# Moving a block of transposes into an earlier phase, and letting two interleaved streams end in step

## The chip, the cores and the metric

The kernel runs on one core of one Trainium2 chip. The metric is the device time of one execution in microseconds (us). PE is the matmul engine, PEld its weight loads, ACT, DVE and POOL are the scalar, vector and GpSimd engines, SP is the engine that issues most of the transfers.

## The reference

One layer of a hybrid decoder, for a prompt of 1024 tokens and for 8 samples of 8 new tokens with 8192 cached positions each. Everything is 32-bit floating point.

```python
h = rmsnorm(x, g_pre_mix) * (1 + sc1) + sh1            # adaLN from c
z = h @ w_in                                           # q, k, v, r, gate of GLA; cq, ckv, kr of MLA
o_a = gla(q_a, k_a, v_a, log_a, s0)                    # gated linear attention, chunks of 64
cq  = rmsnorm(cq, g_mla_q);  ckv = rmsnorm(ckv, g_mla_kv);  kr = rope(kr)
q_nope, q_rope = split(cq @ w_mla_uq);  q_lat = q_nope @ w_mla_uk
s = q_lat . kv_all + q_rope . kr_all                   # causal; a sample: 8192 cached rows, then its 8
o_b = rmsnorm((softmax(scale * s) @ kv_all) @ w_mla_uv, g_mla_out)
x = x + gt1 * rmsnorm(concat(o_a, o_b) @ w_o, g_post_mix)
u = (rmsnorm(x, g_pre_ffn) * (1 + sc2) + sh2) @ w_ffn_up
x = x + gt2 * rmsnorm((conv(u)[a] * gelu(conv(u)[g])) @ w_ffn_down, g_post_ffn)
```

Outputs are both `x`, the new latent rows and rotary keys, the GLA states and the last rows of `u`.

## The kernel before

A matmul of full precision is split: each operand becomes a rounded high part (a cast on ACT, `split` and lines like it) and a low part (a subtraction, `lo`, L121, on DVE or POOL), and three matmuls (`mm3`, L140 to L142) take the place of one.

The program goes through these stages. `phase1` computes `z` for all tokens and stores its parts in scratch memory: the latent rows with their rotary keys in `s_kv` (prompt rows 0 to 1023, sample rows behind them), the query latents stay in SBUF as `cqT`. `sample_queries` makes the samples' queries. Then a mixed stage runs two streams together. `out_proj`, `ffn_up` and `ffn_down` follow it.

*The two streams of the mixed stage.* `run` hands two generators to `interleave` (L1665). The *sample stream* is `mla_sample`: for each of 8 samples, 4 rounds over 2048 cached rows. A round gathers two tiles `L` and two tiles `R` by indirect loads on POOL's queue, transposes them on PE (`kps`, L1222, 40 transposes, copied by ACT at L1224 into `KT` and `KR`), makes the scores `S` (L1232, L1234), takes a softmax on DVE and ACT (L1237 to L1255), transposes the probabilities on DVE (L1261) and multiplies them with `L` (`O`, L1266). The *main stream* is `main` in `run`: `prompt_queries`, then `gla`, then `mla_prompt`, then `out_weights`, which starts the loads of `w_o`.

*What sets the order.* A planner orders each engine's instructions. Each instruction has a priority, a number that counts up as the program is written down, and of those that can go, the lowest number goes first. `interleave` steps the generator that has done the smaller share of its total; a step yields its cost, and the totals are 429.0 for the sample stream and 250.0 for the main one. While it steps the sample stream it adds 450 to the running priority, so that a sample instruction stands as if 450 instructions later; for the main stream it adds 0. An engine's queue and SP's queue run in order: what stands behind a waiting instruction waits too.

*Prompt queries.* `prompt_queries` (L1000) takes tokens in blocks of 256, 256 and 320. `queries` first splits the block of `cqT` into `cqsh` and `cqsl` (`split_cq`, L890; the cast is L132, the subtraction L121 on POOL), with one buffer each, which the matmuls of the whole block read. After each step of the queries one step of `mla_new` follows, which attends to the samples' own 8 new rows; it has six steps, and the queries have 19.

*Prompt attention.* `mla_prompt` (L1029) opens three pools (`mk`, `mb`, `mv`) on the left-hand stack of SBUF where GLA's were, and begins with the keys: 8 times it loads 128 rows of `s_kv` into `kvl` (L1047, two buffers), transposes three 128 x 128 blocks on PE into one PSUM buffer (`pt`, L1050), casts them on ACT into `kTh` (L1051) and subtracts on DVE into `kTl` (L121). Each of these two tiles takes 12 KB of a partition. For each of 4 heads, `keys(h)` loads a part of `w_mla_uk` (`ukr`, L1066), splits it (`uks`, L1059) and makes K; `scores(h, m)` makes the scores of 256 queries (`sps`) and their exponentials `p` (four buffers of 4 KB); `values` transposes `p` on PE (`pt`, L1153), splits the result into `pth` (ACT, L1156) and `ptl` (DVE), and multiplies it with V (`olps`). `values` runs one `scores` behind, so that the last two `values` come after the last scores.

*The hand-over.* `out_weights` opens the pools `fw0` and `fw1` where the prompt attention's pools end, at the same base of the stack. `block` loads a quarter of `w_o` (1 MB) into `uraw` (L1383, two buffers of 8 KB, first in the pool), casts it on ACT into `uhi` (L1388) and subtracts on DVE into `ulo`; the first block's `uhi` and `ulo` come next in the pool. A tile can be written only when what lay at its addresses is done with. `out_proj` loads the mixed rows (`mx`, L1414), transposes them (`tps`, L1421) and multiplies them with the four blocks (`y`); after it come the blocks of `w_ffn_up`, which use the same two raw buffers.

Of the kernel before, what the change touches and what calls it, by code (L numbers as in the profile page):

```python
# [1 line left out]

# [1 line left out]

# [5 lines left out]
F32 = mybir.dt.float32  # L11
F32R = mybir.dt.float32r
# [8 lines left out]
P = 128  # L21
D = 1024
TP = 1024
# [82 lines left out]
class Kernel:  # L106
# [781 lines left out]
            self.lo(self.uk[1][:, o], p3, self.uk[0][:, o], nc.vector)  # L888

    def split_cq(self, c0, n, eng=None):  # L890
        return self.split(self.qp, self.cqT[:, :, c0:c0 + n], (3, 320), "cqs", eng, bufs=1, n=n)

    def queries(self, qp, pp, c0, n, rope, ql=None, cqs=None):

# [102 lines left out]
            except StopIteration as e:  # L997
                return e.value

    def prompt_queries(self):  # L1000

        new = self.mla_new(self.kp, self.nq, self.pq, self.qs, self.qrs)
        for c0, n in ((0, 256), (256, 256), (512, 320)):
            gen = self.queries(self.qp, self.pq, c0, n, self.ropet[:, c0 // P:])
            while True:
                try:
                    yield next(gen)
                except StopIteration as e:
                    self.store_queries(*e.value, c0, n)
                    break  # L1010
                next(new, None)
        for _ in new:
            pass
# [15 lines left out]
    def mla_prompt(self):  # L1029
        nc, A = self.nc, self.A  # L1030
        with ExitStack() as es:
            kp = es.enter_context(self.pool("mk"))
            bp = es.enter_context(self.pool("mb", bufs=1))
            mv = es.enter_context(self.pool("mv"))
            ep = self.ep
            psS = es.enter_context(self.pool("pss", bufs=2, space=PSUM))
            pq = es.enter_context(self.pool("psq", bufs=1, space=PSUM))
            causal = kp.tile([P, P], F32R, name="causal")
            craw = kp.tile([P, P], F32, name="craw")
            nc.sync.dma_start(craw, A["c_causal"])  # L1040
            nc.scalar.copy(causal, craw)
            kTh = kp.tile([P, 3, TP], F32R, name="kTh")
            kTl = kp.tile([P, 3, TP], F32R, name="kTl")
            for i in range(8):
                kv = bp.tile([P, 3, P], F32, name="kvl", tag="kvl", bufs=2)
                o = slice(i * P, (i + 1) * P)
                nc.sync.dma_start(kv.rearrange("p c k -> p (c k)"), self.s_kv[o])  # L1047
                ps = pq.tile([P, 3, P], F32, name="pt", tag="Q", bufs=1)
                for c in range(3):
                    nc.tensor.transpose(ps[:, c], kv[:, c], self.ident)  # L1050
                nc.scalar.copy(kTh[:, :, o], ps)  # L1051
                self.lo(kTl[:, :, o], ps, kTh[:, :, o], nc.vector)
                yield 0.4

            def split2(x, name):

                n = x.shape[2]
                t = bp.tile([P, TP], F32R, name=name, tag="pp", bufs=4)[:, 0:4 * n].rearrange("p (j a n) -> p j a n", j=2, a=2)
                nc.scalar.copy(t[:, 0], x)  # L1059
                self.lo(t[:, 1], x, t[:, 0], nc.vector)  # L1060
                return t
# [603 lines left out]
    def interleave(self, *gens):  # L1665

        live = [[0.0, total, g, ahead] for g, total, ahead in gens]
        while live:
            it = min(live, key=lambda x: x[0] / x[1])
            p = self.tc.cur_priority  # L1670
            try:
                self.tc.cur_priority = p + it[3]
                it[0] += next(it[2])
            except StopIteration:
                live.remove(it)
            self.tc.cur_priority -= it[3]


    def run(self, stop=None):
        nc = self.nc  # L1680
        with ExitStack() as es:
            dp = es.enter_context(self.pool("scratch", space=DRAM))
            self.s_kv = dp.tile([T, LAT + 2 * RO], F32, name="s_kv")
            self.s_qn = dp.tile([4, P, TP], F32, name="s_qn")
            self.s_qr = dp.tile([2, P, TP], F32, name="s_qr")
            self.s_qk = dp.tile([4, P, T], F32, name="s_qk")
            self.s_la = dp.tile([T, 256], F32, name="s_la")
            self.s_v = dp.tile([T, 512], F32, name="s_v")
            self.s_r = dp.tile([T, 512], F32, name="s_r")
            self.s_mix = dp.tile([T, D], F32, name="s_mix")  # L1690
            self.s_x2 = dp.tile([T, D], F32, name="s_x2")
            self.s_gate = dp.tile([2, 65, D], F32, name="s_gate")
            self.s_g = dp.tile([NCH, P, T], F32, name="s_g")
            self.s_ml = dp.tile([1, 512], F32, name="s_ml")
            self.cp = cp = es.enter_context(self.pool("const"))
            self.constants(cp)
            self.ada_start(cp)
            fs = es.enter_context(ExitStack())
            gs = es.enter_context(ExitStack())
            ds = es.enter_context(ExitStack())  # L1700
            with ExitStack() as zs, ExitStack() as xs:
                self.zp = zs.enter_context(self.pool("z"))
                self.xp = xs.enter_context(self.pool("x", bufs=2, side="right"))
                self.phase1()
                if stop == "z":
                    return
                with ExitStack() as es2:
                    self.sample_queries(zs, xs, ds, es2)
                    if stop == "q":
                        return  # L1710

                    def main():
                        yield from self.prompt_queries()
                        zs.close()
                        yield from self.gla()
                        yield from self.mla_prompt()
                        self.wp = [fs.enter_context(self.pool(f"fw{j}")) for j in range(2)]
                        self.gt = gs.enter_context(self.pool("gate"))
                        self.out_weights()
                        yield 0.0  # L1720

                    self.ep = es2.enter_context(self.pool("me", bufs=1, side="right"))
                    self.interleave((self.mla_sample(es2), 429.0, 450), (main(), 250.0, 0))
            if stop == "mix":
                return
            with ExitStack() as hs:
                with self.pool("pt", bufs=2, space=PSUM) as self.pt, self.pool("pu", space=PSUM) as self.pu:
                    hT = self.out_proj(hs, ds)
                    gs.close()
                    if stop == "wo":  # L1730
                        return
                    self.ffn_up(hT)
                    if stop == "up":
                        return
            self.ffn_down()
# [35 lines left out]
```

## Time and profile before

| | us |
|---|---|
| three runs of the kernel before | 1873.49, 1874.45, 1879.61 |
| their median | 1874.45 |
| the profiled execution | 1877.98 |
| its span, first to last instruction | 1876.2 |

The profile is of one execution. Its page has the busy time of each engine, the chain of work that ended last, and the costliest groups of instructions; its trace can be asked for stretches of time, for one tile, for waits, and for the instructions of one engine in order of time. Matmuls overlap in it, so that the times of single ones can't be added up; an engine's busy time counts overlaps once. The granted clock is a share of TensorE's full clock, 2.4 GHz; at half of it the engine runs at 1.2 GHz.

### The profile page before, as it was taken

What the parts mean: (1) busy time and instruction counts of PE and PEld (TensorE: products, weight loads), DVE (VectorE), ACT (ScalarE), POOL (GpSimd) and SP (SyncE); (2) the same over time, 40 slices, a digit from 0 to 9 for tenths busy, and PEclk for the clock granted to TensorE, in tenths of its full rate; (3) what the DMA queues carried; (4) which work ended last, traced back from release to release, by engine and by line L of the source; (5) the groups of instructions that cost most, each with busy time, mean ns of one, the idle gap of its engine ahead of it and who ended that gap; (6) DMA issues with size and microseconds to landing.
All of it is one profiled execution on the core that took longest, in us unless ns stands there. A gap on an engine that the chain in (4) does not pass through costs nothing.

```text
span 1876.2 us, 30747 instructions
## 1 busy us (share of the span) xinstructions
PE 1804.7 (96%) x12403; PEld 1501.0 (80%) x12403; DVE 933.5 (50%) x1680; ACT 709.3 (38%) x1398; POOL 528.5 (28%) x567
## 2 busy tenths in 40 slices
PE   6999999999998999999889999999999999999998
PEld 3888767766654677776589999999999999888787
DVE  4740234358873555565546855455555554623433
ACT  3451111465655667566523422222222222323322
POOL 2640100334443223232101223333333331202221
PEclk7999999999999999999989999999999999999999
DMA  8255653665556555455543312112211112834563
GB/s 308 75 163 181 195 159 100 216 212 189 174 194 213 174 191 179 141 167 192 180 147 116 131 64 71 70 69 71 69 56 64 69 62 71 255 110 115 159 188 95
DMA packets 170617, 265.26 MB, mean 141 GB/s; under 512 B 18277, under 2 KB 118693, under 8 KB 162282
## 3 DMA queue, kind: packets, MB, share of 16 engines
q1 hardware_dynamic: 156138, 179.39, 29.5%
q0 software_dynamic: 14336, 83.89, 12.9%
q8 instruction: 98, 1.61, 0.4%
q14 instruction: 45, 0.37, 0.1%
HBM read 221.49 MB, written 41.75 MB: 140 GB/s over the span
## 4 chain that ended last, share of the span: by engine, by line
PE 84%; DMA 6%; DVE 4%; ACT 4%; issue 1%; POOL 1%; SPq 0%; DVEq 0%; POOLq 0%; ACTq 0%
PE ups L140 9%; PE ups L142 9%; PE ups L141 9%; PE kps L1222 6%; PE yps L142 4%; PE yps L140 4%; PE yps L141 4%; PE zps L140 3%; PE zps L142 3%; PE zps L141 3%; PE O L1266 3%; PE S L1232 3%; PE y L140 2%; PE y L141 2%; PE y L142 2%; PE adaps L248 2%
## 5 line engine op out<-in xcount | busy, mean ns | idle before, releaser
L140 PE MATMUL ups<-gh,uhi 128*128 128x384 f32 (+1 forms) x1056 | 347.4, 329 | 0.3 <-DVE hraw L342 0.3
L141 PE MATMUL ups<-gl,uhi 128*128 128x384 f32 (+1 forms) x1056 | 346.9, 328 | 0.0
L142 PE MATMUL ups<-gh,ulo 128*128 128x384 f32 (+1 forms) x1056 | 346.7, 329 | 0.0
L1560 DVE TENSOR_SCALAR cv<-u,vt 128x1024 f32<-128x1024 f32 (+1 forms) x88 | 133.1, 1533 | 216.0 <-ACT u L1550 179.0
L140 PEld LDWEIGHTS ups<-gh,uhi 128*128 128x128 f32 x1056 | 198.4, 188 | 0.7 <-DVE hraw L342 0.6
L142 PEld LDWEIGHTS ups<-gh,ulo 128*128 128x128 f32 x1056 | 198.4, 188 | 0.1
L141 PEld LDWEIGHTS ups<-gl,uhi 128*128 128x128 f32 x1056 | 198.4, 188 | 0.0
L1224 ACT COPY KT<-kps 128x512 f32<-128x512 f32 x256 | 145.6, 590 | 84.0 <-PE kps L1222 82.4
L121 POOL TENSOR_TENSOR ulo<-uraw,uhi 128x2048 fp32r<-128x2048 f32 x24 | 111.4, 4641 | 207.5 <-ACT uhi L1388 204.7
L1222 PEld LDWEIGHTS kps<-ident,L 128*128 128x128 f32 x1024 | 113.3, 143 | 64.0 <-issue 43.3
L1222 PE MATMUL kps<-ident,L 128*128 128x128 f32 x1024 | 156.9, 283 | 7.9 <-ACT KT L1224 6.4
L1550 ACT COPY u<-ups 128x384 f32<-128x384 f32 (+1 forms) x130 | 57.6, 444 | 278.8 <-PE ups L142 278.8
L142 PE MATMUL yps<-uhi,gl 128*128 128x512 f32 x341 | 132.8, 390 | 5.0 <-DVE gl L121 5.0
L140 PE MATMUL yps<-uhi,gh 128*128 128x512 f32 x341 | 132.7, 389 | 0.0
L141 PE MATMUL yps<-ulo,gh 128*128 128x512 f32 x341 | 132.6, 389 | 0.0
L121 DVE TENSOR_TENSOR gl<-graw,gh 128x1408 fp32r<-128x1408 f32 x31 | 59.0, 1908 | 128.3 <-ACT gh L1607 128.3
L1213 POOL DMA_INDIRECT R<-cache_krope,idx x64 | 64.9, 1014 | 184.1 <-PE kps L1222 141.8
L1607 ACT CAST gh<-graw 128x1408 fp32r<-128x1408 f32 (+1 forms) x35 | 45.7, 1307 | 157.1 <-PE yps L141 127.6
L1388 ACT CAST uhi<-uraw 128x2048 fp32r<-128x2048 f32 (+1 forms) x38 | 70.7, 1864 | 89.7 <-PE ups L141 67.2
L1212 POOL DMA_INDIRECT L<-cache_latent,idx x64 | 63.6, 993 | 136.3 <-PE O L1266 63.7
L140 PE MATMUL zps<-whi,hh 128*128 128x512 f32 (+2 forms) x256 | 96.3, 376 | 0.0
L142 PE MATMUL zps<-whi,hl 128*128 128x512 f32 (+2 forms) x256 | 94.2, 368 | 0.8 <-DVE hl L121 0.8
(443 smaller groups left out, 3802.8 us busy)
## 6 DMA issues: line engine op xcount, KB each, us to landing
wraw<-w_ada SPq DMA_DIRECT2D x48, 512.0 KB
uraw<-w_ffn_up SPq DMA_DIRECT2D x22, 1024.0 KB
graw<-s_g SPq DMA_DIRECT2D x32, 704.0 KB
s_g<-gl SPq DMA_DIRECT2D x22, 544.0 KB
uraw<-w_ffn_down SPq DMA_DIRECT2D x10, 1024.0 KB
xt<-x_prompt SPq DMA_DIRECT2D x16, 512.0 KB
wraw<-w_in SPq DMA_DIRECT2D x12, 512.0 KB
uraw<-w_o SPq DMA_DIRECT2D x4, 1024.0 KB
```

Source lines behind the costliest of these rows:

```text
L121: eng.tensor_tensor(out, x, hi.bitcast(F32), ALU.subtract)
L140: mm(out, wh, xh, start=start, stop=False)
L141: mm(out, wh, xl, start=False, stop=False)
L142: mm(out, wl, xh, start=False, stop=stop)
L1212: nc.gpsimd.indirect_dma_start(L.rearrange("p j l -> p (j l)"), None, cl, io)
L1213: nc.gpsimd.indirect_dma_start(R.rearrange("p j l -> p (j l)"), None, ck, io)
L1222: nc.tensor.transpose(ps[:, k], x, self.ident)
L1224: nc.scalar.copy(KT[:, q // 2, j0:j0 + 4] if q < 4 else KR[:, 4 * half:4 * half + 4], ps)
L1232: nc.tensor.matmul(S[r], Q[:, c], KT[:, c, :, r], start=(c == 0), stop=False)
L1388: self.nc.scalar.copy(hi, raw)
L1550: copy(u[:, 2 + c0:2 + c0 + m], ps[:, 0:m])
L1560: nc.vector.tensor_scalar(yv[z], sh(2)[z], self.cw2[:, ch:ch + 1], self.cb[:, ch:ch + 1], ALU.mult, ALU.add)
```

## The change

The keys of the prompt attention become a generator of their own, `prompt_keys`, with the same loads, transposes, casts and subtractions. `prompt_queries` chains it behind `mla_new`, so that its eight tiles are written down among the steps of the queries, before GLA. `kTh` and `kTl` lie in a new pool `mkT` on the right-hand stack of SBUF, `kvl` in the pool of the queries (two buffers, as before), and the transposes use the four PSUM buffers of the queries instead of the one buffer of the prompt attention. `mla_prompt` starts with the keys of the first head. The split query latents get two buffers each. `interleave` scales what it adds to the priority by the share of the stream that is still to come: 450 at first, 0 at the end. The main stream's total becomes 244.5.

```diff
     def split_cq(self, c0, n, eng=None):
-        return self.split(self.qp, self.cqT[:, :, c0:c0 + n], (3, 320), "cqs", eng, bufs=1, n=n)
+        return self.split(self.qp, self.cqT[:, :, c0:c0 + n], (3, 320), "cqs", eng, bufs=2, n=n)
...
+    def prompt_keys(self, kp, bp, pq):
+        nc = self.nc
+        self.kTh = kp.tile([P, 3, TP], F32R, name="kTh")
+        self.kTl = kp.tile([P, 3, TP], F32R, name="kTl")
+        for i in range(8):
+            kv = bp.tile([P, 3, P], F32, name="kvl", tag="kvl", bufs=2)
+            o = slice(i * P, (i + 1) * P)
+            nc.sync.dma_start(kv.rearrange("p c k -> p (c k)"), self.s_kv[o])
+            ps = pq.tile([P, 3, P], F32, name="qps", tag="Q")
+            for c in range(3):
+                nc.tensor.transpose(ps[:, c], kv[:, c], self.ident)
+            nc.scalar.copy(self.kTh[:, :, o], ps)
+            self.lo(self.kTl[:, :, o], ps, self.kTh[:, :, o], nc.vector)
+            yield
...
-    def prompt_queries(self):
-        new = self.mla_new(self.kp, self.nq, self.pq, self.qs, self.qrs)
+    def prompt_queries(self, keys):
+        new = chain(self.mla_new(self.kp, self.nq, self.pq, self.qs, self.qrs), keys)
...
     def mla_prompt(self):
+            kTh, kTl = self.kTh, self.kTl
...
-            kTh = kp.tile([P, 3, TP], F32R, name="kTh")
-            kTl = kp.tile([P, 3, TP], F32R, name="kTl")
-            for i in range(8):
-                kv = bp.tile([P, 3, P], F32, name="kvl", tag="kvl", bufs=2)
...
-                ps = pq.tile([P, 3, P], F32, name="pt", tag="Q", bufs=1)
...
-                yield 0.4
...
     def interleave(self, *gens):
-                self.tc.cur_priority = p + it[3]
+                late = int(it[3] * (1.0 - it[0] / it[1]))
+                self.tc.cur_priority = p + late
...
+                    mk = es2.enter_context(self.pool("mkT", side="right"))
                     def main():
-                        yield from self.prompt_queries()
+                        yield from self.prompt_queries(self.prompt_keys(mk, self.nq, self.pq))
...
-                    self.interleave((self.mla_sample(es2), 429.0, 450), (main(), 250.0, 0))
+                    self.interleave((self.mla_sample(es2), 429.0, 450), (main(), 244.5, 0))
```

## Rows read from the trace of the kernel before

**Rows 1.** The page, first part: busy us of each engine, share, instructions.

```profile
PE 1804.7 (96%) x12403; PEld 1501.0 (80%) x12403; DVE 933.5 (50%) x1680; ACT 709.3 (38%) x1398; POOL 528.5 (28%) x567
```

**Rows 2.** Stretches: length, busy us (instructions) by engine, clock, DMA share, GB/s.

```profile
core 0: us, PE busy (x) PEld busy (x) DVE busy (x) ACT busy (x) POOL busy (x), PEclk, DMA share, GB/s
345.00:400.00 55.00, 51.70 (x435) 38.09 (x434) 20.04 (x65) 25.13 (x53) 15.22 (x14) 0.97 0.47 155
...
577.00:622.00 45.00, 37.66 (x338) 23.16 (x331) 15.91 (x50) 22.80 (x52) 12.76 (x15) 0.92 0.71 239
622.00:880.00 258.00, 253.08 (x2213) 183.81 (x2212) 139.74 (x406) 165.55 (x405) 74.20 (x97) 1.00 0.49 165
880.00:926.00 46.00, 40.73 (x365) 27.78 (x367) 20.03 (x58) 26.02 (x56) 8.79 (x11) 0.96 0.60 207
926.00:960.00 34.00, 24.23 (x213) 17.86 (x206) 16.68 (x27) 12.39 (x21) 0.94 (x2) 0.85 0.67 229
960.00:1000.00 40.00, 40.00 (x339) 39.66 (x338) 24.59 (x41) 12.38 (x23) 6.38 (x14) 1.00 0.30 103
```

**Rows 3.** PE in order of time: start, us, instruction, [idle before, releaser].

```profile
378.23 0.74 PE L140 MATMUL qps<-cqsh,uqh 128*128 128x320 f32 x3 [2.54 <-ACT cqsh L132]
...
588.02 0.55 PE L1050 MATMUL pt<-ident,kvl 128*128 128x128 f32 x3 [1.92 <-DMA kvl<-s_kv]
590.72 1.06 PE L1276 MATMUL fps<-small,on 128*128 128x32 f32 x4 [2.16 <-DVE on L1271]
...
880.34 0.39 PE L1123 MATMUL sps<-kTl,qrs 128*128 128x512 f32 x1
...
892.55 0.39 PE L140 MATMUL olps<-pth,vh 128*128 128x256 f32 x1 [3.67 <-ACT pth L1156]
...
925.40 0.28 PE L142 MATMUL olps<-pth,vl 128*128 128x128 f32 x1
...
942.06 3.54 PE L1266 MATMUL O<-L,pt 128*32 128x256 f32 x32 [6.99 <-DVE pt L1261]
...
948.63 0.47 PE L140 MATMUL y<-uhi,mh 128*128 128x256 f32 x1 [0.24 <-ACT mh L1423]
```

**Rows 4.** ACT in order of time.

```profile
377.19 0.99 ACT L132 CAST cqsh<-cqT 128x960 fp32r<-128x960 f32 x1
...
588.93 0.40 ACT L1059 CAST uks<-ukr 128x256 fp32r<-128x256 f32 x1 [2.69 <-DMA ukr<-w_mla_uk]
...
890.11 1.90 ACT L1388 CAST uhi<-uraw 128x2048 fp32r<-128x2048 f32 x1 [1.95 <-DMA uraw<-w_o]
891.92 0.58 ACT L1156 CAST pth<-pt 128x512 fp32r<-128x512 f32 x1
```

**Rows 5.** The tile `kvl`: ns (min/median/max), first and last start; idle time before.

```profile
L1050 PE MATMUL pt<-ident,kvl x24: 272/273/477, 588.0 to 617.4; 128*128 128x128 f32 x24
...
  DMA kvl<-s_kv: 5.1, 3
```

**Rows 6.** DVE in order of time.

```profile
937.58 2.29 DVE L121 TENSOR_TENSOR ulo<-uraw,uhi 128x2048 fp32r<-128x2048 f32 x1 [0.55 <-ACT uhi L1388]
```

**Rows 7.** The tile `kTh`, columns as in rows 5.

```profile
L140 PE MATMUL sps<-kTh,uks x16: 389/397/501, 606.1 to 833.0; 128*128 128x512 f32 x16
...
L1051 ACT CAST kTh<-pt x8: 478/485/535, 590.7 to 618.3; 128x384 fp32r<-128x384 f32 x8
L121 DVE TENSOR_TENSOR kTl<-pt,kTh x8: 557/558/558, 591.3 to 618.9; 128x384 fp32r<-128x384 f32 x8
```

**Rows 8.** The chain that ended last, in order of time: start, us, what.

```profile
608.57 6.36 DMA kvl<-s_kv
...
930.50 5.13 DMA uraw<-w_o
```

**Rows 9.** SP's queue in order of time: transfers issued.

```profile
880.94 1.03 SPq L1383 DMA_DIRECT2D uraw<-w_o  x2
...
939.90 0.37 SPq L1383 DMA_DIRECT2D uraw<-w_ffn_up  x1
940.32 1.05 SPq L1414 DMA_DIRECT2D mx<-s_mix  x2
```

More of the change, by code (lines that the diff above doesn't have):

```diff
@@ L2 @@
 from contextlib import ExitStack, contextmanager
+from itertools import chain
 import numpy as np
@@ L1041, in mla_prompt @@
             nc.scalar.copy(causal, craw)
-            kTh = kp.tile([P, 3, TP], F32R, name="kTh")
-            kTl = kp.tile([P, 3, TP], F32R, name="kTl")
-            for i in range(8):
-                kv = bp.tile([P, 3, P], F32, name="kvl", tag="kvl", bufs=2)
-                o = slice(i * P, (i + 1) * P)
-                nc.sync.dma_start(kv.rearrange("p c k -> p (c k)"), self.s_kv[o])
-                ps = pq.tile([P, 3, P], F32, name="pt", tag="Q", bufs=1)
[L1049 to L1052, printed above, removed]
-                yield 0.4
             def split2(x, name):
@@ L1675, in interleave @@
                 live.remove(it)
-            self.tc.cur_priority -= it[3]
+            self.tc.cur_priority -= late
     def run(self, stop=None):
```

## Prediction

> **What bounds the kernel now.** I read the page first: PE is busy for 96% of the span [rows 1], so I looked for the places where it is not. The change touches only the mixed stage, roughly 345 to 960 us, in which two streams share the core: the *sample stream* (`mla_sample`, 32 rounds of attention over the cache) and the *main stream* (prompt queries, GLA, prompt attention, then the loads of `w_o`). The view by stretches shows what there is to win: PE idle is the length less PE's busy time [rows 2]. It is 55.00 - 51.70 = 3.3 us in the queries, 45.00 - 37.66 = 7.3 where GLA hands over to prompt attention, only 258.00 - 253.08 = 4.9 in all of prompt attention, 46.00 - 40.73 = 5.3 in its last stretch and 34.00 - 24.23 = 9.8 at the exit. The granted clock takes more: one minus the mean clock, times the length, is 0.03 x 55 = 1.7, 0.08 x 45 = 3.6, 0.04 x 46 = 1.8 and 0.15 x 34 = 5.1 us [rows 2]. So the stage is bound by PE's own work except at these places. Reordering work inside the full stretch (622 to 880) can win little; closing the holes can win some 38 us at the very most, and only in part.
>
> The waits and timelines say what each hole is. In the queries PE waited 2.54 us for `cqsh` (378.23 [rows 3]), a copy that ACT made at 377.19 [rows 4]. At the hand-over PE stood before `pt<-kvl` for 1.92 us, waiting for a load, and then 2.16 us for DVE (588.02 and 590.72 [rows 3]); ACT had stood 2.69 us for the load of `ukr` (588.93 [rows 4]) with everything behind it. Over the whole run the eight key tiles made engines wait three times on their load, 5.1 us in all [rows 5]. At 892.55 PE waited 3.67 us for `pth` [rows 3], because ACT first waited for a `w_o` load and then cast it (890.11, then `pth` at 891.92 [rows 4]). The longest wait of all, 6.99 us, is at 942.06 [rows 3]: the sample's last softmax, behind a 2.29 us subtraction of `w_o` on DVE (937.58 [rows 6]).
>
> **The change, part by part.** *Prompt keys.* The same work is moved: 24 transposes of 273 ns median, overlapping (three take 0.55 us, 588.02 [rows 3]), so 8 x 0.55 = 4.4 us of PE, 8 casts of 0.485 = 3.9 us of ACT, 8 subtractions of 0.558 = 4.5 us of DVE [rows 5, 7], and 8 loads on SP's queue. The sum of PE's work does not change. In the queries ACT has about 30 us free and DVE 35 of 55 [rows 2], so the casts hide. The eight loads are now queued on SP among the stores of the queries; there are still two `kvl` buffers, so a load starts when the transposes two tiles earlier are done, and a late one stops PE's queue, the queries' matmuls and the sample's transposes behind it. Bounds for the waits there: 0, and 5.1 us as in the old place [rows 5]. One such load held the chain for 6.36 us [rows 8], and the DMA share here, 0.47, is below the 0.71 of the old place [rows 2]; so I take the middle, 2.5 us.
> The Trainium skill (DMA: Bandwidth & Descriptors, Anatomy of one DMA) gives a transfer about 2.0 us fixed plus bytes over 436 GB/s; as an estimate from that page, 192 KB would be 2.5 us, two tiles ahead would always be enough, and the sum below would be 2.5 us lower. The 6.36 us row does not agree with it in this kernel.
>
> *Two buffers for `cqs`.* The split of the next query block no longer waits for the last matmul that reads the one before. That takes away the 2.54 us wait and, I think, the low clock behind it (the 0.97 of this stretch [rows 2]). Win: 2.5 + 1.7 = 4.2, at least 0 (ACT may still be late with it, for it also waited for a GLA load just before). Queries together: 4.2 - 2.5 = 1.7 us won, between 5.0 won and 5.1 lost.
>
> *Hand-over, 577 to 622.* What stays is the load of `ukr`, which ACT waits for, in the same burst of loads, now two `kvl` loads shorter. What goes is the wait before `kvl` and the seven tiles that follow; K of the first head, whose first matmul is now at 606.1 [rows 7], can start as soon as `ukr` is split. Of 7.3 + 3.6 = 10.9 us I take half, 5.5. Lower bound 2 (only the 1.92 us wait), upper bound 10.9.
>
> *Order at the end, 880 to 926.* The left-hand SBUF is a stack: the prompt attention's pools end, and the pool of the `w_o` blocks starts at the same base. Before, the first thing in it is 24 KB of `kTh` and `kTl` per partition, dead after the last scores: the first `w_o` load starts at 880.94 [rows 9], right behind the prompt's last matmul over `kTl` (880.34 [rows 3]), and so ACT gets its cast before the last two `values` are done. After, the keys lie on the right, everything slides down by 27 KB (with the `kvl` buffers), and the first block's `uhi` and `ulo` (16 to 32 KB from the base) fall on the four `p` buffers (10 to 26 KB), which the last `values` read. So the cast can't come ahead of `pth` any more: the 3.67 us and the low clock go. Win 3.7 + 1.8 = 5.5, between 0 and 7.1 (all that this stretch loses).
>
> *Exit, 926 to 960.* The lag was 450 instructions throughout and now falls to zero at the end, so the sample should end with the main stream, not 20 us after it: its last `O` is at 942.06, the main stream's last value matmul at 925.40 [rows 3]. That is two-sided. The late sample round covers the hand-over to `out_proj`: from 925.40 to the first `y` at 948.63 [rows 3] are 23.2 us, in which PE is busy for some 24.2 - 11.4 = 12.8 (the busy time of 926 to 960 less what follows `y`'s start [rows 2]); 10.4 us and the clock's 5.1 are lost. After, all four `w_o` blocks are split when the main stream is done. With 1.90 a cast, 2.29 a subtraction and 5.13 a load [rows 4, 6, 8], two raw buffers and loads in order, the first is ready after 4.2 us, the second, whose raw buffer also lies on `p`, after 5.1 + 4.2 = 9.3, and the fourth, which needs that buffer, after 9.3 + 5.1 + 4.2 = 18.6, against the 937.58 + 2.29 - 925.40 = 14.5 of now [rows 3, 6]. The 96 matmuls of the first tile's `y` take 96 x 40 / 339 = 11.3 us [rows 2]. If `y` follows each block as it comes, its last quarter ends at 18.6 + 2.8 = 21.4 us, of which 21.4 - 11.3 - 1.1 (the transposes before it) = 9.0 are lost against 15.5 now: 6 won. If `y` starts as late as now with nothing to cover it, 16 are lost (below). I take 3 lost.
>
> *Elsewhere*, in GLA and the full stretch, the smaller lag reorders work between streams that together fill PE. I put 0, give or take 4, about the idle time of 622 to 880.
>
> **Sum.** -1.7 - 5.5 - 5.5 + 3.0 = -9.7 us. The profiled execution took 1877.98 us (a span of 1876.2 and 1.8 around it); it lies 3.5 above the median of the three runs shown, 1874.45, inside their range. 1877.98 - 9.7 = 1868.3; by the median it is 1874.45 - 9.7 = 1864.8, and since two of three runs lie there I say 1865.
>
> **Rivals.**
> *No change.* The holes are moved, not closed: `kvl` waits in the queries as long as it did (5.1 lost against 4.2 won), the hand-over still waits for `ukr`, winning 2. With 5.5 at 880 and 3 lost at the exit: -3.6, 1871. For it: ACT's wait of 2.69 us for `ukr` [rows 4] is untouched. Against it: the wait for `cqsh` has a cause that goes.
> *Slower: the sample ends first.* With no lag, the sample's last score matmuls come before the main stream's last two `values`. These then run alone, seven rounds in which PE waits for a copy and a subtraction, 7 x (0.58 + 0.56) = 8.0 us [rows 4, 7], and nothing covers the exit. There `mx` was loaded only at 940.32, behind the second `w_ffn_up` load at 939.90 [rows 9], which waits for the fourth split; 8.3 us later came `y` (948.63 [rows 3]). So 18.6 + 0.5 + 8.3 = 27.4 us from the last values to `y`, idle but for 1.1: 26.3 lost against 10.4 now, 16 more. Together 24 lost, against the 12.7 won before the exit: 1874.45 + 11.3 = 1886. It decides from the point where the sample's last `S` is done before the last but one `values` begins. Against it: the two streams are given out in proportion, so they should end within a round.
> *More is won.* The streams end together, `mx` is loaded early, `y` follows the blocks as they come: the exit wins 6 instead of losing 3: -18.7, so 1856.
> That the smaller lag does nothing is possible too; it leaves the exit at 0 and lies inside the forecast.
>
> **Numbers.** A measurement of this kernel can tell about 0.3%, 5.6 us, from no change. Chances: forecast 0.45 (1858 to 1869), no change 0.26, more 0.14, slower 0.15. The range 1854 to 1879 takes in the first three and the poor bounds of the queries and the exit; it leaves out the worst of the slower case and the best of the better. Faster 0.45 + 0.14, less a little for the forecast's upper edge, 0.57; same 0.27; slower 0.16.
>
> **What would show it.** Right: no PE wait for `cqsh`; K's first matmul near 590 rather than 606; no `uhi` cast of `w_o` on ACT before the main stream's last `pth`; the last `O` within a few us of the last value matmul. Wrong: PE waits for `kvl` between 345 and 400 beyond 3 us; a hole before K as long as now; more than 25 us from the last value matmul to the first `y`; or new holes between 622 and 880, which would mean that the lag's order matters where I put nothing.

## The result, and the profile after

The changed kernel takes 1861.56 us (median of 4 runs, 1861.26 to 1864.08) where the kernel before takes 1875.85 (4 runs): a ratio of 0.9922, 95% interval 0.9907 to 0.9937, or 14.3 us less. The profiled execution took 1861.26, its span is 1859.5. Line numbers are one higher than before up to the queries and five higher from the sample attention on.

The first part of the page of the changed kernel, against [rows 1]:

```profile
PE 1797.6 (97%) x12403; PEld 1500.4 (81%) x12403; DVE 930.1 (50%) x1680; ACT 708.9 (38%) x1398; POOL 529.8 (28%) x567
```

The view by stretches of the changed kernel, columns as in [rows 2]. The last two cuts are its last `values` matmul (907.5) and its first `y` (927.7):

```profile
320.00:345.00 25.00, 21.99 (x162) 19.23 (x161) 11.40 (x31) 14.75 (x35) 12.82 (x11) 0.93 0.82 294
345.00:400.00 55.00, 53.86 (x482) 41.59 (x481) 21.64 (x71) 27.34 (x59) 10.81 (x10) 1.00 0.56 188
400.00:577.00 177.00, 170.33 (x1834) 105.92 (x1836) 126.73 (x335) 107.17 (x232) 84.41 (x92) 0.99 0.59 196
577.00:622.00 45.00, 41.76 (x392) 25.70 (x385) 19.05 (x57) 27.20 (x61) 16.64 (x17) 1.00 0.71 243
622.00:880.00 258.00, 255.73 (x2317) 188.59 (x2315) 143.50 (x419) 172.68 (x420) 78.44 (x102) 1.00 0.52 173
880.00:907.50 27.50, 26.92 (x269) 19.44 (x265) 12.01 (x36) 16.01 (x34) 3.27 (x5) 1.00 0.46 158
907.50:927.70 20.20, 9.28 (x75) 5.06 (x74) 12.35 (x21) 10.27 (x14) 0.93 (x2) 0.69 0.63 217
927.70:960.00 32.30, 31.30 (x235) 30.65 (x235) 13.00 (x23) 6.07 (x11) 1.60 (x4) 0.88 0.50 178
```

Stretches of the kernel before that [rows 2] do not have, its last `values` matmul at 925.4 and its first `y` at 948.6:

```profile
320.00:345.00 25.00, 22.79 (x176) 19.98 (x175) 11.58 (x32) 13.95 (x34) 9.51 (x9) 0.93 0.91 322
400.00:577.00 177.00, 169.70 (x1874) 107.89 (x1868) 131.91 (x339) 111.94 (x239) 84.72 (x91) 1.00 0.57 190
880.00:925.40 45.40, 40.18 (x356) 27.46 (x355) 19.66 (x57) 25.42 (x54) 8.79 (x11) 0.96 0.61 210
925.40:948.60 23.20, 13.46 (x135) 7.15 (x134) 12.21 (x23) 11.35 (x20) 0.94 (x2) 0.85 0.76 247
```

What a stretch loses is its length less PE's busy time, and one minus the clock, times the length. Worked out so from these rows, from [rows 2], and from the same view of two of the experiments below, in us (idle + clock, or idle alone where the clock was 1.00; differences taken before rounding; "V" is the last `values` matmul, "Y" the first `y`):

| stretch | before | after | lag alone | keys alone | predicted change | found |
|---|---|---|---|---|---|---|
| 320 to 345 | 2.2 + 1.8 | 3.0 + 1.8 | 2.7 | 3.9 + 1.8 | 0 | +0.8 |
| 345 to 400, queries | 3.3 + 1.7 | 1.1 | 3.4 | 2.9 + 1.7 | -1.7 | -3.8 |
| 400 to 577, GLA | 7.3 | 6.7 + 1.8 | 4.3 + 1.8 | 3.6 | 0 | +1.1 |
| 577 to 622, hand-over | 7.3 + 3.6 | 3.2 | 4.8 | 3.7 | -5.5 | -7.7 |
| 622 to 880 | 4.9 | 2.3 | 3.8 | 5.2 | 0 | -2.6 |
| 880 to V | 5.2 + 1.8 | 0.6 | 3.2 | 1.0 | -5.5 | -6.5 |
| V to Y, exit | 9.7 + 3.5 | 10.9 + 6.3 | 3.5 + 0.8 | 15.5 + 7.2 | +3 | +4.0 |
| Y to 960 | 0.1 + 1.7 | 1.0 + 3.9 | 2.1 + 4.2 | 1.5 | (in the exit) | +3.1 |
| sum | 54.1 | 42.5 | 34.6 | 48.0 | -9.7 | -11.6 |

The table finds 11.6 of the 14.3 us. For the lag alone it finds 19.5 where 14.2 were measured, for the keys alone 6.1 of 10.5: it says where the time went, and is good to about 5 us in its sum.

PE of the changed kernel in order of time, columns as in [rows 3]:

```profile
593.25 1.07 PE L1237 MATMUL S<-KT,Qd 128*32 128x512 f32 x8 [0.75 <-ACT ML L1285]
...
600.49 0.66 PE L1227 MATMUL kps<-ident,L 128*128 128x128 f32 x4 [0.79 <-ACT KT L1229]
...
608.52 1.09 PE L1227 MATMUL kps<-ident,L 128*128 128x128 f32 x8
609.37 0.47 PE L141 MATMUL sps<-kTh,uks 128*128 128x512 f32 x1
...
907.49 0.27 PE L143 MATMUL olps<-pth,vl 128*128 128x128 f32 x1
...
908.57 1.05 PE L1239 MATMUL S<-KR,Qd 128*32 128x256 f32 x16
...
916.70 3.64 PE L1271 MATMUL O<-L,pt 128*32 128x256 f32 x32 [6.71 <-DVE pt L1266]
...
925.87 1.97 PE L1426 MATMUL tps<-ident,mx 128*128 128x128 f32 x8 [2.34 <-DMA mx<-s_mix]
927.72 0.58 PE L141 MATMUL y<-uhi,mh 128*128 128x256 f32 x1
```

At the hand-over, K of the first head does not come earlier (606.1 before [rows 7], 609.37 now). A round of the sample stream (`kps`, `S`) stands where PE waited; the longest wait there is 0.79 us. At the end, the sample's last scores (908.57) and the last `values` (907.49) are within 1.1 us of each other. Then the same wait as in [rows 3] is back: the last `O` waits 6.71 us, and the first transposes of `mx` 2.34.

ACT of the changed kernel in order of time (the last `pth`, and the first cast of `w_o`):

```profile
904.65 0.48 ACT L1161 CAST pth<-pt 128x384 fp32r<-128x384 f32 x1 [0.33 <-PE pt L1158]
...
911.53 1.89 ACT L1393 CAST uhi<-uraw 128x2048 fp32r<-128x2048 f32 x1
```

DVE of the changed kernel, with the last softmax's transposition behind a subtraction of `w_o`, like that of [rows 6]:

```profile
913.74 2.29 DVE L122 TENSOR_TENSOR ulo<-uraw,uhi 128x2048 fp32r<-128x2048 f32 x1
915.94 0.70 DVE L1266 STREAM_TRANSPOSE pt<-p 128x512 f32<-128x512 f32 x1
```

SP's queue of the changed kernel. Where a line stands for two issues (x2), its length has the wait for the second in it:

```profile
600.76 0.42 SPq L1071 DMA_DIRECT2D ukr<-w_mla_uk  x1
...
894.00 11.05 SPq L1388 DMA_DIRECT2D uraw<-w_o  x2
913.85 0.37 SPq L1178 DMA_DIRECT2D s_mix<-ob  x1
916.05 3.29 SPq L1388 DMA_DIRECT2D uraw<-w_o  x2
919.44 1.01 SPq L1419 DMA_DIRECT2D mx<-s_mix  x2
```

The chain of work of the changed kernel at the exit (start, us, what):

```profile
914.35 1.59 issue
915.94 0.70 DVE pt L1266
916.75 2.21 DVE ulo L122
918.98 5.58 DMA uraw<-w_o
924.64 1.91 ACT uhi L1393
926.57 2.10 DVE ulo L122
928.77 0.69 DVE ml L122
929.51 1.11 PE tps L1426 x4
```

So the exit goes through the third and fourth block of `w_o`, whose loads wait for raw buffers, and `mx` stands behind these loads on SP. The first `y` (927.7) does not wait for the fourth block, which is split only at 928.9, but for `mx`.

The tile `kvl` of the changed kernel, engines idle before it, against [rows 5]:

```profile
L1012 PE MATMUL qps<-ident,kvl x24: 272/273/332, 363.6 to 390.7; 128*128 128x128 f32 x24
...
  issue: 0.6, 2
```

No engine waits for a load of the keys in their new place.

### The profile page after: what moved, and what is told of

It reads as the page before. It is cut to its first block, busy times and chain, and to the rows that moved or that the text cites. A ratio compares the mean times of both kernels' runs of the same rounds, so it can differ in the third digit from the quotient of the medians.

```text
span 1859.5 us, 30758 instructions
## 1 busy us (share of the span) xinstructions
PE 1797.6 (97%) x12403; PEld 1500.4 (81%) x12403; DVE 930.1 (50%) x1680; ACT 708.9 (38%) x1398; POOL 529.8 (28%) x567
## 3 DMA queue, kind: packets, MB, share of 16 engines
q1 hardware_dynamic: 156138, 179.39, 29.8%
## 4 chain that ended last, share of the span: by engine, by line
PE 70%; DVE 3%; DMA 2%; ACT 1%; issue 1%; SPq 0%; POOL 0%; DVEq 0%; POOLq 0%; ACTq 0%
PE ups L141 9%; PE ups L143 9%; PE ups L142 9%; PE kps L1227 6%; PE yps L143 4%; PE yps L141 4%; PE yps L142 4%; PE S L1237 3%; PE O L1271 3%; PE y L141 2%; PE y L143 2%; PE y L142 2%; PE S L1239 1%; PE lps L705 1%; PE sps L141 1%; PE sps L142 1%
## 5 line engine op out<-in xcount | busy, mean ns | idle before, releaser
L1571 POOL TENSOR_TENSOR gl<-gl,cv 128x1088 f32<-128x1088 f32 x22 | 56.0, 2544 | 135.3 <-ACT gl L1570 135.3
```

Source lines behind the costliest of these rows:

```text
L1571: nc.gpsimd.tensor_tensor(gl, gl, res[0], ALU.mult)
```

## The experiments

The theory at the start was the prediction's: the keys' move closes the hand-over and the stretch at 880, the two buffers close the queries, the smaller lag costs 3 us at the exit. The first rival was that the smaller lag does it. All ratios are to the kernel before, run on the same chip.

**One part at a time.** *Keys alone*: the change without the two edits below.

```diff
-                late = int(it[3] * (1.0 - it[0] / it[1]))
+                late = it[3]
-        ... "cqs", eng, bufs=2, n=n)
+        ... "cqs", eng, bufs=1, n=n)
```

> Only the keys are moved: written down among the steps of the queries, on the right-hand stack, main total 244.5; the lag stays 450 throughout and the split query latents keep one buffer. Theory of the prediction: this part carries +2.5 (waits for key loads in the queries), -5.5 (hand-over) and -5.5 (order at 880 to 926), so -8.5 us, a ratio of 0.9955, with K's first matmul near 590 and no half clock between 577 and 622. Rival 1 (the smaller lag does it): the hand-over keeps a hole for the load of ukr and the ratio lies within 0.2% of 1. Rival 2 (the place in SBUF is what counts): the hand-over keeps its hole, but the last pth is not behind a cast of w_o any more: about -4 to -5 us, 0.9975.

Measured: 0.9945 (0.9932 to 0.9958), -10.5 us. The hand-over loses 3.7 us at full clock in place of 10.9, K begins at 598.7, the stretch up to the last `values` (908.5) loses 1.0. That is the prediction's gain, a little larger. But the main stream now ends 17 us earlier than before and the sample stream only 14: its last `O` starts 19.2 us behind the last `values` (16.7 before) and waits longest of all. `mx` goes out after the second load of `w_ffn_up`, as it did before [rows 9]. PE and SP of the keys alone:

```profile
927.62 3.64 PE L1271 MATMUL O<-L,pt 128*32 128x256 f32 x32 [9.99 <-DVE pt L1266]
```

```profile
926.97 3.36 SPq L1388 DMA_DIRECT2D uraw<-w_ffn_up  x2
930.42 1.00 SPq L1419 DMA_DIRECT2D mx<-s_mix  x2
```

From V to Y this kernel loses 22.8 us, 9.5 more than before: the exit gives back much of what the keys win.

*Lag alone*: the kernel before with the new `interleave`.

```diff
-                self.tc.cur_priority = p + it[3]
+                late = int(it[3] * (1.0 - it[0] / it[1]))
+                self.tc.cur_priority = p + late
```

> Only the lag of the sample stream falls from 450 to 0; keys and buffers as before. Theory of the prediction: +3 at the exit and 0 elsewhere, so between 1.000 and 1.003, with the longest waits at the hand-over (ukr, kvl) unchanged. Rival 1 (the smaller lag does it): the sample's last O moves to within 10 us of the last value matmul, the stretch from the last value matmul to the first y loses 3 us or more, and idle time in 577 to 880 falls by 5 us or more: -8 to -14 us, a ratio of 0.993 to 0.996.

Measured: 0.9924 (0.9911 to 0.9937), -14.2 us, as much as the whole change. The prediction's step (+3) is refuted, the rival holds, though with another exit than it said. The view by stretches of the lag alone, its last `values` matmul at 922.4 and its first `y` at 927.5:

```profile
577.00:622.00 45.00, 40.24 (x407) 24.21 (x405) 19.23 (x61) 27.48 (x60) 17.45 (x18) 1.00 0.71 246
...
880.00:922.40 42.40, 39.16 (x372) 26.55 (x370) 23.23 (x65) 26.02 (x58) 5.81 (x9) 1.00 0.52 179
922.40:927.50 5.10, 1.57 (x13) 1.20 (x12) 3.02 (x3) 4.80 (x6) 0.00 (x0) 0.85 0.69 194
```

The hand-over closes with the keys still in their old place (four rounds of `O` start between 577 and 622, three before). And the exit is 5.1 us long in place of 23.2. SP's queue of the lag alone shows why: `mx` goes out 7 us before the last `values` matmul, and the last `w_o` load behind it.

```profile
915.32 0.92 SPq L1414 DMA_DIRECT2D mx<-s_mix  x2
...
927.22 0.38 SPq L1383 DMA_DIRECT2D uraw<-w_o  x1
```

The sample's last scores start at 911.46 there, after the last but one `values` (ended at 907.3) and ahead of the last one: half of the case of the prediction's slower rival. The stretch loses 3.2 us up to V (8.0 had been the price for both), and the exit gets shorter, not longer.

*Buffers alone*: `bufs=2` for `cqs` in the kernel before.

> Only the split query latents get two buffers each. Theory of the prediction: PE's wait of 2.5 us for cqsh and the low clock behind it go, -4.2 us, a ratio of 0.998. Rival: ACT is late with the cast anyway, or the time won is lost again before the hand-over: 0, within 0.1%.

Measured: 0.9980 (0.9971 to 0.9989), -4.4 us; the term was -4.2. The queries of the buffers alone, against [rows 2]:

```profile
345.00:400.00 55.00, 53.13 (x469) 39.91 (x471) 19.47 (x66) 24.06 (x51) 13.45 (x15) 1.00 0.48 163
```

*Keys and buffers, lag 450 throughout*: the changed kernel with `late = it[3]`.

> The changed kernel with the lag of 450 throughout: keys and buffers without the smaller lag. Theory of the prediction: -12.7 us, 0.9932, faster than the changed kernel by 3 us. Rival 1 (the smaller lag does it): within 4 us of the kernel before, 0.998 or more, with the sample's last O 15 us or more after the last value matmul. If the parts add up, its gain is that of the keys alone and the buffers alone together; if it is over 3 us away from their sum, they share a hole.

Measured: 0.9978 (0.9968 to 0.9988), 12 runs from 1868.18 to 1880.45. The prediction's sum is refuted; without the smaller lag, keys and buffers together are no faster than the buffers alone. The exit is that of the keys alone (29.8 us from V to Y, 14.6 of them busy). Why the two together fall behind the keys alone (0.9945) is open: the profiled run is the fastest of the twelve and shows a stage like that of the keys alone.

**What the keys add to the lag.** *Lag and buffers*: the kernel of the lag alone with `bufs=2`.

> The kernel before with the smaller lag and the two buffers, the keys left where they were. Since the lag alone gave 0.9924, as much as the whole change: if the keys' move adds nothing once the lag shrinks, this is at or below the changed kernel, 0.990 to 0.9925, with the first y within 6 us of the last value matmul. If the keys' move is needed for the whole, this is 3 us or more above the changed kernel, 0.994 and up. The sum of the prediction's terms would be -4.2 + 3 = -1.2, 0.9994.

Measured: 0.9908 (0.9893 to 0.9922). With the keys in their old place it is no slower than the changed kernel: once the lag shrinks and the queries have their buffers, no gain from the keys' move is found. The exit is 9.2 us long, with a wait of 2.75 for `mx`.

*No lag at all*: the changed kernel with `late = 0`.

> The changed kernel with no lag at all: the sample stream has the same priority as the main one from the start. If the end value of the lag is what counts: within 2 us of the changed kernel (0.991 to 0.9935). If the lag is needed early, where a sample round would wait for its gathered tiles on PE: new waits of kps for L and R before 577, and 4 us or more above the changed kernel (0.994 and up). The prediction put the lag's order elsewhere at 0, give or take 4.

Measured: 0.9941 (0.9928 to 0.9953), 0.0015 to 0.0023 or 3 to 4 us above the changed kernel (0.9918 to 0.9926), at the lower bound of the second case; the intervals overlap. Its reason is not shown: between 345 and 960 no wait of `kps` for its gathered tiles is among the large ones. Before 345 one `kps` waits 3.6 us for something that the profile does not name, and 320 to 345 loses 10.8 us; but there the kernel of the lag and the buffers loses 11.1, with a lag that is near 450 so early. What PE waited for in 345 to 960 (in all, times, longest):

```profile
PE tps L1426 <- DMA mx<-s_mix: 6.5, 1, 6.5
PE O L1271 <- DVE pt L1266: 6.3, 7, 2.3
PE kps L1227 <- ACT KT L1229: 5.9, 14, 1.1
PE qps L1012 <- DMA kvl<-s_kv: 3.3, 1, 3.3
```

Here a key load does hold the queries, for 3.3 us, the wait that the prediction had feared at 2.5. The exit is better than the changed kernel's: the last `O` follows the last `values` (926.1) at once, and Y comes after 12.5 us in place of 20.2, held by the wait of 6.5 for `mx`.

```profile
926.54 1.93 PE L1271 MATMUL O<-L,pt 128*32 128x256 f32 x32 [0.19 <-DVE pt L1266]
```

*Lag below zero*: 450 down to -225, with the keys as in "keys below" further down.

```diff
-                late = int(it[3] * (1.0 - it[0] / it[1]))
+                late = int(it[3] * (1.0 - 1.5 * it[0] / it[1]))
```

> The kernel with the keys below the sample's pools, and the lag falling from 450 past zero to -225, so that the sample stream ends ahead of the main one. If the exit is long because the sample's last softmax stands behind subtractions of w_o (6.7 us of waiting for O in the changed kernel): the last O comes before the last value matmul, that wait is gone, and the time is 3 us or more below the changed kernel's, a ratio of 0.990 or less. The rival of the prediction, the sample ends first: the last values then run without cover and nothing covers the exit, 3 us or more above the changed kernel, 0.9935 or more. In between: what the exit wins the last values lose.

Measured: 0.9931 (0.9915 to 0.9947). Neither case happened: the last `O` still starts 9.2 us behind the last `values` matmul and still waits 6.71 us, as in the changed kernel. So below zero the end value of the lag moves nothing. The lag does place the last round, but its end value alone does not tell where: with the keys in their new place the last `O` starts 19.2 us behind the last `values` when the lag stays at 450, 9.2 when it falls to 0 or to -225, and 0.5 when it is 0 throughout.

**The exit.** The move of the keys changes two things in SBUF. On the left, the first blocks of `w_o` fall on `p` (a step of the prediction). On the right, not foreseen: the pool of the keys was opened ahead of the sample's, so that the sample's `KT` slides down 24 KB, onto the buffers of `mx` and `mh` of `out_proj`. This is read from the order of the pools in the program; the traces show no addresses.

*A pad on the left*, so that `w_o` falls on nothing that is in use:

```diff
+            kp.tile([P, 6, TP], F32, name="pad")
             causal = kp.tile([P, P], F32R, name="causal")
```

> The changed kernel with 24 KB of each partition left free under the prompt attention's left-hand pools, so that the first two w_o loads and the first cast again fall on nothing that the last values still read. Theory now (the move of the keys took away the place where w_o could be split early, and that costs the exit): the first uhi cast comes before 900 instead of at 911.5, no subtraction of w_o stands in front of the sample's last softmax, the 6.7 us wait of O shrinks below 3, the first y comes 6 us or more earlier than at 927.7: 5 to 9 us below the changed kernel, a ratio of 0.988 to 0.9895. The prediction's step (an early cast of w_o delays the last pth and costs 5.5 between 880 and 926): 3 to 6 us above the changed kernel, 0.994 to 0.9955. Rival: mx, still behind the w_o loads on SP, holds the first y as before: within 2 us of the changed kernel.

Measured: 0.9956 (0.9942 to 0.9971), some 6 us above the changed kernel (0.9918 to 0.9926, below). The prediction's size and sign hold, the theory of the expectation falls. But the place is another: from V to Y (942.1) this kernel loses 21.6 us, the changed one 17.2. The first cast, now at 885.5, does not hurt the `values` (880 to 919.1 loses 1.3). The second and third cast come at the exit, ahead of the last softmax, and two subtractions with them. ACT and PE of the padded kernel:

```profile
919.68 3.70 ACT L1394 CAST uhi<-uraw 128x2048 fp32r<-128x2048 f32 x2
...
927.54 0.69 ACT L1256 ACTIVATE p<-S,nm 128x512 f32<-128x512 f32 x1 [2.96 <-DVE nm L1253]
```

```profile
929.19 3.50 PE L1272 MATMUL O<-L,pt 128*32 128x256 f32 x32 [8.45 <-DVE pt L1267]
```

*A pad on the right*, in the kernel of the lag alone, where the changed kernel has its keys:

```diff
+                    es2.enter_context(self.pool("mkT", side="right")).tile([P, 6, TP], F32, name="pad")
                     self.ep = es2.enter_context(self.pool("me", bufs=1, side="right"))
```

> The kernel with only the smaller lag, and 24 KB of each partition left free on the right-hand stack where the changed kernel has its keys; nothing else moves. Theory now: KT falls on mx here too, mx is issued at least 5 us later than the 7 us ahead of the last value matmul at which it went with the lag alone, and y starts 10 us or more behind the last value matmul in place of 5.1: 4 to 9 us above the lag alone, a ratio of 0.995 to 0.997. Rival (where KT lies does not matter, for mx waits for s_mix and for SP's queue): within 2 us of the lag alone, 0.991 to 0.9935.

Measured: 0.9957 (0.9941 to 0.9972), 0.0033 or 6.2 us above the lag alone. The order of all instructions is that of the lag alone but for the exit, where `mx` goes out at 928.52 in place of 915.32. SP and PE of this kernel:

```profile
928.52 0.96 SPq L1414 DMA_DIRECT2D mx<-s_mix  x2
```

```profile
933.35 1.97 PE L1421 MATMUL tps<-ident,mx 128*128 128x128 f32 x8 [13.53 <-DMA mx<-s_mix]
```

So the 24 KB cost the early `mx`; that they do it through `KT` is argued from the order of the pools, for the pad moves every pool opened behind it.

*Keys below*: the changed kernel with the pool of the keys opened behind the sample's pools. `KT` is back in its old place, the keys lie over `mx`.

```diff
-                    mk = es2.enter_context(self.pool("mkT", side="right"))
                     def main():
+                        mk = es2.enter_context(self.pool("mkT", side="right"))
```

> The changed kernel with one line moved: the pool of kTh and kTl is opened behind the sample's pools, so that on the right-hand stack the sample's KT stays where it was before the change and the keys lie below it, over mx and mh. Theory now (the move of the keys pushed KT 24 KB down onto the buffers of mx and mh, so that the first load of out_proj waits for the sample's last scores): with the keys dead after the last scores of the prompt, mx is issued before 910, ahead of the third w_o load, its transposes and casts come before the late splits, and the first y comes 5 us or more earlier: 4 to 9 us below the changed kernel of the same call. Rival (the w_o splits and the sample's last softmax hold the exit): mx early, but the first y no earlier than now: within 2 us of the changed kernel.

*The changed kernel again*, on the same chip:

> The changed kernel itself, on the chip of this call, so that the others are compared with it there: 0.991 to 0.9935 by every theory.

Measured: 0.9909 (0.9889 to 0.9929), 1860.78 us, against 0.9918 (0.9903 to 0.9933), 1861.93: no difference to be told. Every engine's instructions stand in the same order in the two, `mx` behind the third and fourth `w_o` load; the last `O` waits 6.7 us in both. So in the changed kernel it is not the place of `KT` that keeps `mx` late. It goes out right behind the fourth `w_o` load on SP; whether another order would let it go earlier was not shown, as the next run says.

*`mx` first*: blocks three and four of `w_o` written down behind the first `prepare`.

```diff
-        self.wo = [self.block(wo[:, :, 256 * q:256 * q + 256], nc.vector) for q in range(4)]
+        self.wo = [... for q in range(2)]
+        self.wo_late = lambda: [... for q in (2, 3)]
...
+            mixes = [prepare(order[0])]
+            self.wo += self.wo_late()
+            mixes.append(prepare(order[1]))
```

> The changed kernel with the third and fourth block of w_o written down behind the first load of mx, so that on SP mx goes ahead of the w_o loads that wait for a raw buffer. Theory now: mx lands some 5 us earlier, its transposes and casts fill the hole of 910 to 925 and stand ahead of the late splits: 2 to 5 us below the changed kernel, 0.9895 to 0.991. Rival (the sample's last softmax, behind a subtraction of w_o, holds the exit): within 1.5 us of the changed kernel. Third case: y gets to the third block before it is split, and what is won at the front is lost there: within 1.5 us too, but with a wait of y for uhi or ulo.

Measured: 0.9926 (0.9913 to 0.9938). The planner gave out every engine's instructions in the order of the changed kernel, so that this is the changed kernel once more, and the question is not answered.

## Why the prediction came out

The time, 1861.6, lies 3.4 us under the 1865 and inside its own range of 1858 to 1869; the gain, 14.3, is 4.6 more than the 9.7 of the sum. By place every term has its sign: queries -1.7 taken, -3.8 found; hand-over -5.5, -7.7; 880 to the last `values` -5.5, -6.5; exit +3, +7.1 with what the first `y` lose; elsewhere 0, -0.7. By cause they do not hold. Of the four signs of being right, one came as it was put down: no cast of `w_o` before the last `pth`. The wait of 2.54 us for `cqsh` went, though one of 1.3 stayed; K did not begin near 590, and the last `O` came 9.2 us behind the last value matmul.

- *Two buffers.* Right: -4.2 taken, -4.4 measured alone. PE's waits for `cqsh` are 1.3 us in all, at the first block.
- *Waits for keys in the queries.* +2.5 taken, none found in the changed kernel. PE waits for a key load 0.8 us with the keys alone, and 3.3 us with no lag at all. The estimate worked out from the Trainium skill (DMA: Bandwidth & Descriptors, Anatomy of one DMA), whose fit is for transfers from the GpSimd path while these go out on SP, has two tiles ahead always enough; the changed kernel's trace shows no such wait, those two runs do.
- *Hand-over.* The size is right, the mechanism was wrong: "K of the first head ... can start as soon as `ukr` is split", near 590. In the changed kernel the load of `ukr` goes out only at 600.76 and K starts at 609.37. By the trace the hole is filled by a round of the sample stream that stands earlier in PE's queue. Keys alone (3.7 lost) and lag alone (4.8) each close the same hole, and together they cannot close it twice (3.2).
- *880 to 926.* Right that no cast of `w_o` comes ahead of the last `pth` any more (911.53 behind 904.65), and that undoing the placement costs about 6 us. Wrong about where: the padded kernel pays at the exit.
- *Exit and lag.* This is the step that failed: "Exit ... I take 3 lost" and "Elsewhere ... I put 0". The lag was priced as a loss; alone it wins 14.2 us, some 6 at the hand-over and, by the table, 9 at the exit less 4.5 that the first `y` give back. That `mx` could go out ahead of the late `w_o` loads, which takes the exit from 23.2 us to 5.1, stood only in the third rival. The changed kernel does not get that exit: 20.2 us, with `mx` behind the two late blocks of `w_o`. The chain of these blocks I had priced (the fourth ready 18.6 us after the last `values`; it was 926.57 + 2.29 - 907.5 = 21.4), but not that the last softmax would wait behind them: by the trace a cast and a subtraction of `w_o` make some 3 of the 6.71 us that the last `O` waits.
- *What I did not see.* The three parts alone sum to -10.5 - 14.2 - 4.4 = -29.1 us; together they give -14.3. And the keys' new pool shifts other tiles: with the lag alone, 24 KB in that place cost 6.2 us, though taking the shift back in the changed kernel ("keys below") wins nothing that can be told.

Of the rivals, "more is won" (1856) did not come, for the exit won nothing, and "the sample ends first" did not either: the last scores and the last `values` end within a round, as the argument against it had said. So the forecast was near because its places were right, and in part by luck. On top of keys and buffers the smaller lag is worth some 10 us (0.9978 to 0.9922) where a loss of 3 was taken; on top of lag and buffers the keys' move is worth nothing (0.9908 against 0.9918 to 0.9926) where 8.5 were taken. The lag's gain and the keys' are largely the same gain, and the two errors all but cancel. What stays open: why keys and buffers without the lag scatter over 12 us, why the planner keeps `mx` behind the late loads in the changed kernel, and what that kernel's exit would be with `mx` ahead of them.

## What to carry to other kernels

When several edits aim at the same holes, price the holes, and then ask of each edit alone which of them it closes; gains that share a hole don't add. Where one stream's end sets off the next stage, look at the first load of that stage first: which queue it stands in, behind what, and on whose buffers. A pool that is opened earlier on a stack moves all pools behind it, and a tile that lands on another's buffer can be a new wait that no diff shows.

## What the runs showed of the chip that was not expected

Four kernels with every engine's instructions in one order (the changed one, again, with the keys below, and with `mx` first) gave medians of 1860.8 to 1865.4 us, not all on one chip, and ratios of 0.9909 to 0.9926. Their profiles differ most at the entrance of the stage: between 320 and 345, idle time and clock cost 4.8, 4.5, 5.6 and 9.2 us.

The clock's price outlasts the hole. From 927.7 to 960 PE of the changed kernel is busy for 31.30 of 32.30 us, at a granted clock of 0.88: 3.9 us, behind a hole in which the clock was 0.69. It is 0.50 from 927.7 to 932.0, 0.56 from 932.0 to 936.0 and 1.00 from there on, so that the lower level (1.2 GHz) is still there when PE is busy again. The prediction's sum for the new exit has no such term: its 5.1 us of clock are those of 926 to 960 before, and it counts the first tile's `y` at the full clock.
